# Gate and up tiles of a SwiGLU layer as 2x2 blocks by Strassen's scheme, in a hybrid decoder step on Trainium2

## The chip, the cores and the metric

The program runs on one core of one Trainium2 chip. The metric is the device time of one execution in microseconds. The kernel before takes 1314.66 us, the median of three runs (1313.83 to 1316.19). TensorE multiplies, VectorE (DVE), ScalarE (ACT) and GpSimd (POOL) work on tiles of 128 partitions, and SyncE (SP) issues most loads.

## The reference

One layer of a hybrid decoder for 512 prompt tokens and 8 sample tokens with the same weights: windowed attention and RWKV-7 time mixing beside each other, merged by gates, one output projection, then a SwiGLU layer. The change concerns the last two lines before the final norm:

```python
x = x + (merged @ w_out)                                 # 1024 x 1024
hn = rms_norm(x, norm_ffn)
ffn = (silu(hn @ w_gate) * (hn @ w_up)) @ w_down         # 1024 -> 2816 -> 1024
y = rms_norm(x + ffn, norm_final)
```

All is in fp32.

## The kernel before

Activations lie transposed: a feature is a partition, the 520 tokens are columns, in two chunks of CH = 260 (`CS`). A product has 8 k-tiles (KD) of 128 features for 1024 inputs. The 2816 hidden features make 22 tiles (KF); each has a gate tile and an up tile of the weights, 128 x 8 x 128 numbers, and the two together are called a pair here.

TensorE multiplies in fp32r, so each fp32 operand is split into a high part and a rest, and a k-tile costs three matmuls: high x high, high weight x rest, rest of the weight x high (`gemm_chunk`, L535). A weight tile is loaded as `raw` by SP (`wraw`, L512), cast to `whi` by ACT and subtracted to `wlo` by DVE (`wsplit`, L521). So a gate or up tile is 2 chunks x 8 k-tiles x 3 = 48 matmuls of 260 columns, and a pair 96.

The multiplications are a list of `Job`s (L455; the list from L1916 on), which `play` (L549) runs one after another; in the second step of a job it loads the weights of the job after next and splits those of the next one. Each chunk takes one of three PSUM banks with the name `mm`; there are three more with the name `ax` and two `ch`.  When a chunk's product is complete, the job's `post` reads it out on DVE or ACT and so empties the bank.

The order on each engine is the order in which the program records its instructions. Other work (`norm2`, L1761, and `final`) runs as generators beside `play`; `Weave.run` (L433) decides at each `yield` who records next, by a model of the engines' clocks (`Clocks`, L226). All instructions are recorded through one helper, so the profile has them all on L380, and tiles are told apart by their names.

Around the change: `wo_pre` (L1721) loads the residual x2 (8 POOL DMAs) for the output projection, `wo_post` (L1746) adds the product to x2 and makes x2 times the norm's weight as a split pair in the places K0 to 21 of the tiles `fh` and `fl`. The norm's scale per token is not known before all of x2 is there. So the first EARLY = 3 pairs are multiplied with that unscaled vector, and the results are multiplied by the scale (`rsf`) in `gt_post` and `up_post`. Meanwhile `norm2` computes the scale, multiplies (`hf`) and splits the scaled vector per k-tile into `h2h` (ACT) and `h2l` (alternately DVE and POOL); all later pairs use these. For gate: `sl` = (tanh(g/2) + 1) x g; for up: `sl` x u; then half of it is split into `fh` and `fl`, which the down tiles read.

Of the kernel before, what the change touches and what calls it, by code (L numbers as in the profile page):

```python
# [42 lines left out]
EARLY = 3  # L43
# [422 lines left out]
def program(tc, I, O):  # L466
# [82 lines left out]
    def play(jobs, more=None):  # L549
        raws, ws = {0: first_raw, 1: second_raw}, {0: first_w}  # L550
# [1167 lines left out]
    mctx, fctx = ExitStack(), ExitStack()  # L1718
    ff = {}

    def wo_pre():  # L1721
        rctx.close()
        gctx.close()
        xp = pool("x2", ctx)
        ff["x2"] = x2 = xp.tile([128, KD, NT], FP, name="x2")
        for k in range(KD):
            G.dma_start(out=x2[:, k], in_=I["xT"][:, k])
# [18 lines left out]
    def wo_post(n):  # L1746
        def post(ps):
            x2 = ff["x2"]
            for c in range(2):
                V.tensor_tensor(out=x2[:, n, CS[c]], in0=x2[:, n, CS[c]], in1=ps[c][:, :CH], op=ALU.add)  # L1750

            g = feat[:, F_FFN, n:n + 1]
            S.activation(out=ff["h"][:, K0 + n], in_=x2[:, n], func=AF.Copy, scale=g)
            V.scalar_tensor_tensor(out=ff["l"][:, K0 + n], in0=x2[:, n], scalar=g, in1=ff["h"][:, K0 + n].bitcast(FP),
                                   op0=ALU.mult, op1=ALU.subtract)
            sumsq(ff["acc"], x2[:, n], n)
            if n == KD - 1:
                wv.spawn(norm2())
        return post

    def norm2():  # L1761
        mctx.close()
        hp2 = ff["hp2"] = pool("h2", h2ctx, side="right")
        hh2 = ff["hh"] = hp2.tile([128, KD, NT], FR, name="h2h")
        hl2 = ff["hl"] = hp2.tile([128, KD, NT], FR, name="h2l")
# [4 lines left out]
        for k in range(KD):  # L1770
# [4 lines left out]
            wv.set("h2", k)  # L1775
            yield (hl2[:, k],)
# [3 lines left out]
    def up_x(n):  # L1780
        return lambda: ([ff["h"][:, K0 + k] for k in range(KD)], [ff["l"][:, K0 + k] for k in range(KD)]) \
            if n < EARLY else (ff["hh"], ff["hl"])

    def gt_post(n):
        def post(ps):
            xp = ff["xp"]
            t = ff["t", n] = xp.tile([128, NT], FP, name=nm("sl"), tag="sl", bufs=2)
            for c in range(2):
                g = ps[c][:, :CH]
                if n < EARLY:  # L1790
                    gs = xp.tile([128, CH], FP, name=nm("g0"), tag="g0")
                    V.tensor_tensor(out=gs[:], in0=g, in1=ff["rs"][:, CS[c]], op=ALU.mult)
                    g = gs[:]
                S.activation(out=t[:, CS[c]], in_=g, func=AF.Tanh, scale=0.5)
                V.scalar_tensor_tensor(out=t[:, CS[c]], in0=t[:, CS[c]], scalar=1.0, in1=g, op0=ALU.add, op1=ALU.mult)
        return post

    def up_post(n):
        def post(ps):
            t = ff["t", n]  # L1800
            for c in range(2):
                V.tensor_tensor(out=t[:, CS[c]], in0=t[:, CS[c]], in1=ps[c][:, :CH], op=ALU.mult)
            if n < EARLY:
                V.tensor_tensor(out=t[:], in0=t[:], in1=ff["rs"][:], op=ALU.mult)
            S.activation(out=ff["h"][:, n], in_=t[:], func=AF.Copy, scale=0.5)
            V.scalar_tensor_tensor(out=ff["l"][:, n], in0=t[:], scalar=0.5, in1=ff["h"][:, n].bitcast(FP),
                                   op0=ALU.mult, op1=ALU.subtract)
        return post

# [106 lines left out]
    for n in range(KF):  # L1916
        rest.append(Job(I["w_gate"][n], KD, up_x(n), gt_post(n), hold=(lambda: wv.until("rs2")) if n == 0 else None,
                        bank=cbank if n == 0 else None, need={k: ("h2", k) for k in range(KD)} if n == EARLY else {}))
# [17 lines left out]
    for n in range(KD - 1):  # L1936
        for k0 in range(0, KF, 8):
            nk = min(8, KF - k0)
            rest.append(Job(I["w_down"][n][:, k0:k0 + nk], nk, down_x, down_post(n) if k0 + nk == KF else None, k0=k0,
                            first=(k0 == 0), last=(k0 + nk == KF), pre=down_pre if n == 0 and k0 == 0 else None))  # L1940

    for c in range(2):
        for k0 in range(0, KF, 8):
            nk = min(8, KF - k0)
            rest.append(Job(I["w_down"][KD - 1][:, k0:k0 + nk] if c == 0 else None, nk, down_x,
# [4 lines left out]
    wv.run(play(jobs, more))  # L1950
# [17 lines left out]
```

## Time and profile before

| | us |
|---|---|
| median of three runs | 1314.66 |
| profiled execution | 1316.53 |
| its span | 1314.8 |
| TensorE busy | 1264.7 |
| DVE busy | 843.7 |
| ACT busy | 610.6 |
| POOL busy | 175.0 |

The span is what the trace covers of the profiled execution, from the first instruction to the last. Busy times of different engines lie beside each other; a share over the whole span is a mean over stages. The mean granted clock of TensorE in the span is 0.98. In the trace, matmuls of 260 columns start some 0.12 us apart and are shown 0.28 us long, since they are pipelined. A row of the timeline has start, duration, engine, line, operation, output<-inputs with shapes, and in brackets the idle time of the engine before it with what ended it.

### The profile page before, as it was taken

Reading aid. Unit: us, or ns where it says so; the run is one execution under the profiler, and the core shown is the slowest. Engines: PE = TensorE matmul, PEld = TensorE weight load, DVE = VectorE, ACT = ScalarE, POOL = GpSimd, SP = SyncE. Lnnn points to the kernel's source line nnn. Section 1 sums busy time; section 2 is a strip of 40 time slices with the busy share of each in tenths; the row PEclk is TensorE's granted clock in tenths of the full one; section 3 lists DMA queues with packets and bytes.
Section 4 is the critical chain, followed back from the end, with each engine's and each line's share of the span. In section 5 each row is a group of like instructions: output and inputs, shape, how many; then the busy total and the mean of one; then the engine's idle time right before and its main releaser. Section 6 shows DMA issues by size and latency. Waiting matters only on the chain.

```text
span 1314.8 us, 29468 instructions
## 1 busy us (share of the span) xinstructions
PE 1264.7 (96%) x11738; PEld 1197.5 (91%) x11738; DVE 843.7 (64%) x2221; ACT 610.6 (46%) x1554; POOL 175.0 (13%) x261
## 2 busy tenths in 40 slices
PE   7999999999989989999999999999999999999996
PEld 7998999989978878888888888999999999999996
DVE  6956866954869998886986665555843444332333
ACT  5244244366656656675785665334433232222220
POOL 1300100100223332121123122110200000000000
PEclk9999999999989999997999999999999999999998
DMA  6523654634245554543245454552222222223331
GB/s 215 158 94 96 213 178 146 221 112 172 69 131 136 152 147 141 143 156 97 77 139 168 123 175 157 182 192 85 81 97 97 97 89 89 97 93 89 89 101 65
DMA packets 92137, 169.48 MB, mean 129 GB/s; under 512 B 42416, under 2 KB 47568, under 8 KB 92000
## 3 DMA queue, kind: packets, MB, share of 16 engines
q1 hardware_dynamic: 60880, 102.46, 24.6%
q0 software_dynamic: 14512, 46.47, 11.5%
q10 hardware_dynamic: 16608, 18.68, 4.3%
q8 instruction: 92, 1.51, 0.5%
q14 instruction: 45, 0.37, 0.1%
HBM read 133.20 MB, written 27.94 MB: 123 GB/s over the span
## 4 chain that ended last, share of the span: by engine, by line
PE 64%; DVE 15%; issue 9%; DMA 6%; ACT 4%; POOL 1%; SPq 1%; ACTq 0%; DVEq 0%; POOLq 0%
PE mm L380 51%; PE ax L380 8%; PE ch L380 5%; DVE wlo L380 2%; DVE X L380 1%; DVE xt L380 1%; DMA fb<-FD 1%; DMA sw<-raw 1%; ACT KB L380 1%; DVE k L380 1%; DMA raw<-w_in 1%; SPq L380 1%; DVE raw L380 1%; DVE qk L380 1%; DVE GH L380 1%
## 5 line engine op out<-in xcount | busy, mean ns | idle before, releaser
L380 PE MATMUL mm<-hh,whi 128*128 128x260 f32 x1136 | 340.2, 299 | 0.8 <-ACT gt L380 0.8
L380 PE MATMUL mm<-hh,wlo 128*128 128x260 f32 x1136 | 325.4, 286 | 4.3 <-DVE wlo L380 4.3
L380 PE MATMUL mm<-hl,whi 128*128 128x260 f32 x1136 | 325.7, 287 | 0.0
L380 ACT CAST whi<-raw 128x1024 fp32r<-128x1024 f32 (+1 forms) x165 | 170.1, 1032 | 324.4 <-PE mm L380 290.6
L380 DVE TENSOR_TENSOR wlo<-raw,whi 128x1024 fp32r<-128x1024 f32 (+1 forms) x165 | 197.9, 1199 | 140.2 <-ACT whi L380 137.0
L380 PEld LDWEIGHTS mm<-hh,whi 128*128 128x128 f32 x1136 | 215.7, 190 | 13.3 <-issue 6.0
L380 PEld LDWEIGHTS mm<-hh,wlo 128*128 128x128 f32 x1136 | 215.4, 190 | 6.5 <-DVE wlo L380 5.8
L380 PEld LDWEIGHTS mm<-hl,whi 128*128 128x128 f32 x1136 | 215.5, 190 | 1.4 <-issue 0.2
L380 PE MATMUL mm<-h2l,whi 128*128 128x260 f32 x608 | 171.5, 282 | 0.0
L380 PE MATMUL mm<-h2h,wlo 128*128 128x260 f32 x608 | 171.4, 282 | 0.0
L380 PE MATMUL mm<-h2h,whi 128*128 128x260 f32 x608 | 171.4, 282 | 0.0
L380 PEld LDWEIGHTS mm<-h2h,wlo 128*128 128x128 f32 x608 | 114.5, 188 | 0.0
L380 PEld LDWEIGHTS mm<-h2l,whi 128*128 128x128 f32 x608 | 114.4, 188 | 0.0
L380 PEld LDWEIGHTS mm<-h2h,whi 128*128 128x128 f32 x608 | 114.4, 188 | 0.0
L380 PE MATMUL mm<-fh,wlo 128*128 128x260 f32 x388 | 109.6, 282 | 0.0
L380 PE MATMUL mm<-fh,whi 128*128 128x260 f32 x388 | 109.5, 282 | 0.0
L380 PE MATMUL mm<-fl,whi 128*128 128x260 f32 x388 | 109.5, 282 | 0.0
L380 PEld LDWEIGHTS mm<-fh,whi 128*128 128x128 f32 x388 | 73.1, 188 | 0.0
L380 PEld LDWEIGHTS mm<-fl,whi 128*128 128x128 f32 x388 | 73.0, 188 | 0.0
L380 PEld LDWEIGHTS mm<-fh,wlo 128*128 128x128 f32 x388 | 72.9, 188 | 0.0
L380 DVE TENSOR_TENSOR xt<-X,LT 128x60 f32<-128x60 f32 (+24 forms) x248 | 60.3, 243 | 3.6
L380 DVE TENSOR_TENSOR X<-X,xt 128x60 f32<-128x60 f32 (+24 forms) x248 | 57.6, 232 | 3.8
(390 smaller groups left out, 2588.8 us busy)
## 6 DMA issues: line engine op xcount, KB each, us to landing
raw<-w_in SPq DMA_DIRECT2D x77, 512.0 KB, 3.7
raw<-w_gate SPq DMA_DIRECT2D x22, 512.0 KB, 3.2
raw<-w_up SPq DMA_DIRECT2D x22, 512.0 KB, 3.2
raw<-w_down SPq DMA_DIRECT2D x16, 512.0 KB, 3.5
kt<-kcache POOLq DMA_DIRECT2D x24, 256.0 KB, 3.7
kt<-vcache POOLq DMA_DIRECT2D x24, 256.0 KB, 3.5
sw<-raw ACTq DMA_DIRECT2D x64, 65.0 KB, 3.6
GD<-gt ACTq DMA_DIRECT2D x16, 260.0 KB, 3.0
```

What stands on the lines that cost most here:

```text
L380: r = f(*a, **k)
```

## The change

EARLY becomes 4. The pairs 4 to 21 leave the job list for a new generator `pairs`. Of these 18, the pairs 4, 7, 10, 13, 16 and 19 stay plain and are done in four units (gate and up, each in two halves of four k-tiles) of 24 matmuls. The other twelve are taken as a 2x2 block product: rows are the gate tile and the up tile, the inner dimension is the two halves of the k-tiles (A and B), columns are the two chunks. Strassen's scheme in Winograd's form has seven products of 12 matmuls instead of eight, four sums of weight blocks, four sums of blocks of the hidden vector, and seven sums of results. All sums are on DVE.

`norm2` works on pairs of k-tiles j and j + 4: two scaled vectors, one split of four blocks, four block differences, one split of these, each split over 4 x 260 = 1040 columns by one ACT cast and one DVE subtraction; POOL has no part of it. Weights are split per unit, in halves of 512 columns, into four half slots, three units ahead; weight sums are written into `accf`, `rsf` and over the raw tiles. Units take the three `mm` and three `ax` banks by turns. Raw weights of every other pair come into two tiles of their own. To make room, x2 is written to DRAM in `wo_post` (8 POOL DMAs) and loaded again when the down tiles begin (8 POOL DMAs), and part of `fh`/`fl` is made later in memory that x2 had (`fz`).

The diff, cut to its core:

```diff
-EARLY = 3
+EARLY = 4
...
     def wo_post(n):
...
+            G.dma_start(out=X2D[:, n], in_=x2[n])
...
     def norm2():
...
-        for k in range(KD):
-            t = ff["xp"].tile([128, NT], FP, name=nm("hf"), tag="sq", bufs=2)
-            V.scalar_tensor_tensor(out=t[:], in0=ff["x2"][:, k], scalar=feat[:, F_FFN, k:k + 1], in1=ff["rs"][:],
-                                   op0=ALU.mult, op1=ALU.mult)
-            split(hh2[:, k], hl2[:, k], t[:], (V, G)[k % 2])
+        for j in range(KD // 2):
+            z = ff["fp"].tile([128, 8, CH], FP, name=nm("z"), tag=f"z{j % 2}")
+            for i in range(2):
+                k = j + i * KD // 2
+                V.scalar_tensor_tensor(out=z[:, 2 * i:2 * i + 2], in0=ff["x2"][k].rearrange("p (b c) -> p b c", b=2),
+                                       scalar=feat[:, F_FFN, k:k + 1], in1=ff["rs"][:].rearrange("p (b c) -> p b c", b=2),
+                                       op0=ALU.mult, op1=ALU.mult)
+            split(hh2[:, j, :4], hl2[:, j, :4], z[:, :4])
+            for o, x, y in ((4, 1, 0), (6, 3, 1), (5, 3, 4), (7, 2, 5)):
+                V.tensor_tensor(out=z[:, o], in0=z[:, x], in1=z[:, y], op=ALU.subtract)
+            yield (z[:, 7],)
+            split(hh2[:, j, 4:], hl2[:, j, 4:], z[:, 4:])
...
+    def pairs():
...
+        for n in range(EARLY, KF):
+            if (n - EARLY) % 3:
+                units += [(n, True, w, ((b, w, True, True),)) for w, b in enumerate((0, 5, 2, 6, 7, 4, 3))]
+            else:
+                units += [(n, False, w, tuple((b, 2 * (w // 2) + c, w % 2 == 0, w % 2 == 1) for c, b in
+                                              enumerate(((0, 1), (2, 3))[w % 2]))) for w in range(4)]
...
+            out, x, y, op = {1: (s2, s1, g[:, A], ALU.subtract), 3: (u[:, A], g[:, A], u[:, A], ALU.subtract),
+                             6: (g[:, A], g[:, B], s2, ALU.subtract)}.get(w, (None,) * 4)
+            if w == 1:
+                V.tensor_tensor(out=s1, in0=u[:, A], in1=u[:, B], op=ALU.add)
+            if out is not None:
+                V.tensor_tensor(out=out, in0=x, in1=y, op=op)
...
+                S.copy(out=hi, in_=src)
+                V.tensor_tensor(out=lo, in0=src, in1=hi.bitcast(FP), op=ALU.subtract)
...
+            if w == 0:
+                S.copy(out=p, in_=o)
+            elif w == 1:
+                plus(q, p)
+            elif w == 2:
+                plus(p, p)
+                silu2(t[:, CS[0]], p)
+            elif w == 3:
+                plus(r, q)
+            elif w == 4:
+                plus(p, r)
+                V.tensor_tensor(out=t[:, CS[0]], in0=t[:, CS[0]], in1=p, op=ALU.mult)
+            elif w == 5:
+                plus(q, q)
+                plus(r, r)
+            else:
+                plus(q, q)
+                silu2(t[:, CS[1]], q)
+                V.tensor_tensor(out=t[:, CS[1]], in0=t[:, CS[1]], in1=r, op=ALU.mult)
+                half_out(n, t)
...
+        for q in range(3):
+            prep(q)
...
+            prep(q + 3)
...
-    wv.run(play(jobs, more))
+    def everything():
+        yield from play(jobs, {0: first_raw, 1: second_raw}, {0: first_w}, more)
+        yield from pairs()
+        yield from play(down, down_raw, down_w)
+    wv.run(everything())
```

In the order on DVE before, one pair of the long stretch (a row has the line, the operation, output<-inputs and the shape; `mm` are products in PSUM):

```order
L380 TENSOR_TENSOR wlo_13316<-raw_13252,whi_13315 128x1024
L380 SCALAR_TENSOR_TENSOR sl_13295<-sl_13295,mm_13270 128x260
L380 TENSOR_TENSOR sl_13295<-sl_13295,mm_13300 128x260
L380 TENSOR_TENSOR sl_13295<-sl_13295,mm_13331 128x260
L380 TENSOR_TENSOR wlo_13376<-raw_13313,whi_13375 128x1024
L380 SCALAR_TENSOR_TENSOR fl<-sl_13295,fh 128x520
```

In the new order on DVE, about half of a block pair (`pq` are the accumulated results, `mm` and `ax` the products in PSUM, `accf`, `rsf` and `raw` on the left are sums of weight blocks):

```order
L380 TENSOR_TENSOR wlo_13270<-raw_13598,whi_13269 128x512
L380 TENSOR_TENSOR pq_13797<-pq_13797,ax_13815 128x260
L380 TENSOR_TENSOR wlo_13270<-accf,whi_13269 128x512
L380 TENSOR_TENSOR accf<-raw_13673 128x512
L380 TENSOR_TENSOR pq_13797<-pq_13797,mm_13831 128x260
L380 TENSOR_TENSOR wlo_13268<-raw_13597,whi_13267 128x512
L380 SCALAR_TENSOR_TENSOR sl_13796<-sl_13796,pq_13797 128x260
L380 TENSOR_TENSOR pq_13798<-pq_13797,ax_13854 128x260
L380 TENSOR_TENSOR wlo_13268<-raw_13672,whi_13267 128x512
L380 TENSOR_TENSOR rsf<-accf,raw_13672 128x512
L380 TENSOR_TENSOR pq_13797<-pq_13798,mm_13870 128x260
```

Rests of weights and sums of results stand by turns, the sums of weights of the next pair among them.

In the early stretch, before, DVE's rows from the weight rest at 925.83 us to the first product of up tile 0 (`mm_12777`; `g` is a gate product times the scale):

```order
L380 TENSOR_TENSOR wlo_12793<-raw_12712,whi_12792 128x1024
L380 SCALAR_TENSOR_TENSOR hf_12746<-x_12155,feat,rsf 128x520
L380 TENSOR_TENSOR g_1889_12769<-ch_12699,rsf 128x260
L380 SCALAR_TENSOR_TENSOR hf_12796<-x_12155,feat,rsf 128x520
L380 TENSOR_TENSOR h2l<-hf_12746,h2h 128x520
L380 SCALAR_TENSOR_TENSOR sl_12768<-sl_12768,g_1889_12769 128x260
L380 SCALAR_TENSOR_TENSOR hf_12837<-x_12155,feat,rsf 128x520
L380 TENSOR_TENSOR g_1890_12773<-ch_12730,rsf 128x260
L380 TENSOR_TENSOR sl_12768<-sl_12768,mm_12777 128x260
```

And in the new order the same stretch (the product is `mm_12794`; `z` are the blocks and their sums):

```order
L380 TENSOR_TENSOR wlo_12810<-raw_12724,whi_12809 128x1024
L380 SCALAR_TENSOR_TENSOR z_12758<-x_1833_12165,feat,rsf 128x520
L380 SCALAR_TENSOR_TENSOR z_12758<-x_1834_12166,feat,rsf 128x520
L380 TENSOR_TENSOR z_12758<-z_12758 128x260 x3
L380 TENSOR_TENSOR g_1895_12786<-ch_12711,rsf 128x260
L380 TENSOR_TENSOR h2l<-z_12758,h2h 128x1040
L380 TENSOR_TENSOR z_12758<-z_12758 128x260
L380 SCALAR_TENSOR_TENSOR sl_12785<-sl_12785,g_1895_12786 128x260
L380 SCALAR_TENSOR_TENSOR z_12888<-x_1833_12165,feat,rsf 128x520
L380 TENSOR_TENSOR g_1896_12790<-ch_12742,rsf 128x260
L380 TENSOR_TENSOR h2l<-z_12758,h2h 128x1040
L380 SCALAR_TENSOR_TENSOR sl_12785<-sl_12785,g_1896_12790 128x260
```

The next row reads `mm_12794`. Two rests of 1040 columns and the four sums of z now stand ahead of it, in place of one rest of 520 and one scaled vector of 520.

More of the change, by code (lines that the diff above doesn't have):

```diff
@@ L1716, in pb_post @@
         return post
-    mctx, fctx = ExitStack(), ExitStack()
+    mctx, fctx, sctx = (ExitStack() for _ in range(3))
+    X2D = drp.tile([128, KD, NT], FP, name="X2D")
     ff = {}
@@ L1731, in wo_pre @@
         fp = pool("ff", fctx)
-        ff["h"] = fp.tile([128, KF, NT], FR, name="fh")
-        ff["l"] = fp.tile([128, KF, NT], FR, name="fl")
+        for x in "hl":
+            a, b = (fp.tile([128, n, NT], FR, name=nm("f" + x)) for n in (EARLY, KF - EARLY - 8))
+            ff[x] = [a[:, k] for k in range(EARLY)] + [None] * 8 + [b[:, k] for k in range(KF - EARLY - 8)]
+        ff["fp"] = fp
+        xs = [fp.tile([128, 8, CH], FP, name=nm("x2"), tag=f"x{i}") for i in range(2)]
+        ff["x2"] = x2 = [xs[k // 4][:, k % 4 * 2:k % 4 * 2 + 2].rearrange("p a b -> p (a b)") for k in range(KD)]
+        for k in range(KD):
+            G.dma_start(out=x2[k], in_=I["xT"][:, k])
         yield ()
@@ L1763, in norm2 @@
         hp2 = ff["hp2"] = pool("h2", h2ctx, side="right")
-        hh2 = ff["hh"] = hp2.tile([128, KD, NT], FR, name="h2h")
-        hl2 = ff["hl"] = hp2.tile([128, KD, NT], FR, name="h2l")
+        hh2 = ff["hh"] = hp2.tile([128, KD // 2, 8, CH], FR, name="h2h")
+        hl2 = ff["hl"] = hp2.tile([128, KD // 2, 8, CH], FR, name="h2l")
         banks = yield from norm_r(ff["xp"], [ff["acc"]], slice(0, NT), TB, "f")
@@ L1769, in norm2 @@
         wv.set("rs2")
[L1770 to L1776 removed]
+        for j in range(KD // 2):
[10 more added lines that the diff above has]
+            split(hh2[:, j, 4:], hl2[:, j, 4:], z[:, 4:])
+            wv.set("h2", j)
+            yield (hl2[:, j],)
+        for i, x in enumerate("hl"):
+            for o, y in ((EARLY, "z"), (EARLY + 4, "x")):
+                w = ff["fp"].tile([128, 8, CH], FR, name=nm("fz"), tag=f"{y}{i}")
+                ff[x][o:o + 4] = [w[:, 2 * k:2 * k + 2].rearrange("p a b -> p (a b)") for k in range(4)]
+        ff["wp"] = pool("ws", sctx)
+        wv.set("ws")
     h2ctx = ExitStack()
     def up_x(n):
[L1781 to L1782 removed]
+        return lambda: (ff["h"][K0:], ff["l"][K0:])
     def gt_post(n):
@@ L1915, in program @@
         rest.append(Job(I["w_out"][n], KD, lambda: (mrg["h"], mrg["l"]), wo_post(n), pre=wo_pre if n == 0 else None))
-    for n in range(KF):
+    for n in range(EARLY):
         rest.append(Job(I["w_gate"][n], KD, up_x(n), gt_post(n), hold=(lambda: wv.until("rs2")) if n == 0 else None,
-                        bank=cbank if n == 0 else None, need={k: ("h2", k) for k in range(KD)} if n == EARLY else {}))
+                        bank=cbank if n == 0 else None))
         rest.append(Job(I["w_up"][n], KD, up_x(n), up_post(n)))
@@ L1922, in down_x @@
         return ff["h"], ff["l"]
+    down, down_raw, down_w = [], {}, {}
     def down_pre():
+        sctx.close()
         h2ctx.close()
+        ff["x2"] = pool("x2b", ctx, side="right").tile([128, KD, NT], FP, name="x2b")
+        for k in range(KD):
+            G.dma_start(out=ff["x2"][:, k], in_=X2D[:, k])
         yield ()
@@ L1938, in program @@
             nk = min(8, KF - k0)
-            rest.append(Job(I["w_down"][n][:, k0:k0 + nk], nk, down_x, down_post(n) if k0 + nk == KF else None, k0=k0,
+            down.append(Job(I["w_down"][n][:, k0:k0 + nk], nk, down_x, down_post(n) if k0 + nk == KF else None, k0=k0,
                             first=(k0 == 0), last=(k0 + nk == KF), pre=down_pre if n == 0 and k0 == 0 else None))
@@ L1944, in program @@
             nk = min(8, KF - k0)
-            rest.append(Job(I["w_down"][KD - 1][:, k0:k0 + nk] if c == 0 else None, nk, down_x,
+            down.append(Job(I["w_down"][KD - 1][:, k0:k0 + nk] if c == 0 else None, nk, down_x,
                             down_post(KD - 1, (c,)) if k0 + nk == KF else None, k0=k0, first=(k0 == 0),
```

117 lines of the change are left out of this document (97 added, 20 removed).

## The prediction

> **What bounds the kernel now.** I first read the page's busy line and its slices, then a table of the stages, then the timeline of VectorE in one pair of gate and up tiles. The busy line of the page:
>
> ```profile
> PE 1264.7 (96%) x11738; PEld 1197.5 (91%) x11738; DVE 843.7 (64%) x2221; ACT 610.6 (46%) x1554; POOL 175.0 (13%) x261
> ```
>
> The 96% is a mean over stages, so the stages decide. The table of stretches (length, then busy time and count of PE, PEld, DVE, ACT, POOL, then granted clock, DMA share, GB/s):
>
> ```profile
> 820.00:871.00 51.00, 49.61 (x409) 48.79 (x408) 29.04 (x53) 15.26 (x22) 7.51 (x14) 1.00 0.53 177
> 871.00:917.00 46.00, 46.00 (x387) 45.92 (x386) 25.39 (x39) 17.26 (x23) 4.23 (x8) 1.00 0.40 139
> 917.00:926.00 9.00, 8.87 (x75) 8.46 (x74) 4.94 (x16) 3.85 (x6) 0.00 (x0) 1.00 0.17 58
> 926.00:954.30 28.30, 28.30 (x238) 28.30 (x238) 26.18 (x38) 12.34 (x21) 6.81 (x4) 1.00 0.24 85
> 954.30:1172.00 217.70, 217.70 (x1827) 217.70 (x1827) 89.41 (x134) 63.02 (x95) 0.00 (x0) 1.00 0.27 93
> 1172.00:1290.00 118.00, 118.00 (x987) 118.00 (x986) 36.37 (x45) 26.73 (x31) 0.00 (x0) 1.00 0.29 87
> ```
>
> Up to 917 the orders of both kernels agree; 917 to 954 is pairs 0 to 2; 954.3 to 1172 is pairs 3 to 21, 19 of them with 96 matmuls each (1824; the row counts 1827); then come the down tiles. From 926 to 1290 TensorE is busy all the time at clock 1.00. DVE works 89.41 of 217.70 us in the long stretch (41%), ACT 63.02, POOL nothing, DMA 27%. There a matmul less is time less, as long as DVE's added work finds its place. In 926 to 954.3, however, DVE is already busy 26.18 of 28.30 us.
>
> One pair in the long stretch, from the timeline of DVE (start, duration, ..., in brackets the idle time before and what ended it):
>
> ```profile
> 992.29 0.43 DVE L380 SCALAR_TENSOR_TENSOR sl<-sl,mm 128x260 f32<-128x260 f32 x1 [0.54 <-ACT sl L380]
> 995.67 1.23 DVE L380 TENSOR_TENSOR wlo<-raw,whi 128x1024 fp32r<-128x1024 f32 x1 [2.96 <-ACT whi L380]
> ...
> 997.54 0.43 DVE L380 TENSOR_TENSOR sl<-sl,mm 128x260 f32<-128x260 f32 x1 [0.30 <-PE mm L380]
> 1000.39 0.43 DVE L380 TENSOR_TENSOR sl<-sl,mm 128x260 f32<-128x260 f32 x1 [2.43 <-PE mm L380]
> ...
> 1003.75 0.42 DVE L380 SCALAR_TENSOR_TENSOR sl<-sl,mm 128x260 f32<-128x260 f32 x1 [0.55 <-ACT sl L380]
> ```
>
> The same instruction returns after 1003.75 - 992.29 = 11.46 us, so a matmul costs 11.46/96 = 0.1194 us. DVE waits for others in every gap; nobody waits for it.
>
> **What goes: 144 matmuls.** Pairs 4 to 21 are 18 pairs of tiles, six plain and twelve in 2x2 blocks. A block pair has 7 products of 4 k-tiles x 3 = 12 matmuls, 84 in place of 96. The order shows the same: 144 matmuls fewer on TensorE. 144 x 0.1194 = 17.19 us, if TensorE stays without idle time. The Trainium skill ("TensorE: Matmul & The Clock Gate", section "Back-to-back issue gap") has an isolated gap of N/2.4 + 2.5 ns, 110.8 ns for 260 columns, which would make the saving 15.96 us, an estimate from that page; it adds that sustained streams run below this at N=512. The row above is a sustained stream at 0.1194 us, so the row decides.
>
> **What comes on DVE in a block pair.** Durations overlap between neighbours, so I take the distance from start to start of instructions that follow each other without idle time:
>
> ```profile
> 940.17 0.41 DVE L380 TENSOR_TENSOR g<-mm,rsf 128x260 f32<-128x260 f32 x1
> 940.51 1.21 DVE L380 TENSOR_TENSOR wlo<-raw,whi 128x1024 fp32r<-128x1024 f32 x1
> 941.64 0.41 DVE L380 SCALAR_TENSOR_TENSOR sl<-sl,g 128x260 f32<-128x260 f32 x1
> 941.98 1.80 DVE L380 SCALAR_TENSOR_TENSOR hf<-x,feat,rsf 128x520 f32<-128x520 f32 x1
> 943.70 0.41 DVE L380 TENSOR_TENSOR sl<-sl,mm 128x260 f32<-128x260 f32 x1
> 944.04 0.75 DVE L380 SCALAR_TENSOR_TENSOR hf<-x,feat,rsf 128x520 f32<-128x520 f32 x1
> 944.71 0.69 DVE L380 TENSOR_TENSOR h2l<-hf,h2h 128x520 fp32r<-128x520 f32 x1
> 945.32 0.41 DVE L380 TENSOR_TENSOR sl<-sl,mm 128x260 f32<-128x260 f32 x1
> ```
>
> 260 columns take 0.34 (940.17 to 940.51), 520 take 0.61 (944.71 to 945.32), 1024 take 1.13 (940.51 to 941.64), a scaled 520 takes 0.67 (944.04 to 944.71). No row has 512 columns: between 0.34 and 0.61, I take 0.60, nearest to 520. A block pair then costs DVE 7 weight rests x 0.60 + 4 weight sums x 0.60 + 7 output sums x 0.34 + 4 silu and product steps x 0.34 + the final rest 0.61 = 10.95 us, beside 84 x 0.1194 = 10.03 us of TensorE. It is over by 0.92. A plain pair has 4 x 0.60 + 4 x 0.34 + 0.61 = 4.37 us beside 11.46. Three pairs together: DVE 2 x 10.95 + 4.37 = 26.3 us, TensorE 2 x 10.03 + 11.46 = 31.5 (34.4 before). So the sum fits only over three pairs, with DVE 1.8 us behind after two block pairs and 7 us of slack in the plain one. Weight halves are split three products ahead, each with 12 x 0.1194 = 1.43 us, together 4.3 us, and I followed the new order instruction by instruction with these durations: every weight rest is ready 1.9 us or more before TensorE asks for it. The rotation of the six PSUM banks gives no wait there. ACT's steps are, by the rows of the tile h2h and of a group of the long stretch (median, then mean ns),
>
> ```profile
> L380 ACT CAST h2h<-hf x8: 627/628/630, 927.8 to 944.8; 128x520 fp32r<-128x520 f32 x8
> L380 ACT ACTIVATE sl<-mm 128x260 f32<-128x260 f32 x38 | 14.6, 385 | 27.4 <-PE mm L380 27.4
> ```
>
> 7 casts x 0.63 + the copy and two tanh x 0.39 + the final cast 0.63 = 6.2 us of a block pair's 10.03; I cost it at nothing, DVE being the fuller one. The weights are the same bytes, and DMA was at 27%. Term: 0, bounds 0 and +2.
>
> **What comes in the early stretch.** The blocks of the hidden vector and their sums are made while pairs 0 to 3 run: per two k-tiles, two scaled 520s (1.34), four sums (1.36) and two rests of 1040 columns (some 1.15 each by the slope from 520 to 1024), 5.0 us, and four times that 20. Before, DVE had eight scaled 520s and four rests of 520, 7.8 us, and POOL the other four rests. So 12 us more on an engine that was full. POOL's share leaves, and with it its contention with DVE:
>
> ```profile
> 940.99 2.23 POOL L380 TENSOR_TENSOR h2l<-hf,h2h 128x520 fp32r<-128x520 f32 x1 [4.53 <-ACT h2h L380]
> 945.53 1.31 POOL L380 TENSOR_TENSOR h2l<-hf,h2h 128x520 fp32r<-128x520 f32 x1 [2.31 <-ACT h2h L380]
> ```
>
> Beside the first of these the scaled 520 of 941.98 took 1.80 instead of 0.75. DVE stays full from 926 on, now to about 965, 12 us past the old end of the stretch; the fourth early pair lies there. The wait that this makes is that for a PSUM bank. Pairs before 954.37 go half a tile (24 matmuls, 2.87 us) after another:
>
> ```profile
> 925.83 1.23 DVE L380 TENSOR_TENSOR wlo<-raw,whi 128x1024 fp32r<-128x1024 f32 x1 [1.66 <-PE ch L380]
> 931.67 0.41 DVE L380 TENSOR_TENSOR sl<-sl,mm 128x260 f32<-128x260 f32 x1
> ...
> 954.25 0.28 PE L380 MATMUL mm<-fh,wlo 128*128 128x260 f32 x1
> 954.37 0.28 PE L380 MATMUL mm<-h2h,whi 128*128 128x260 f32 x1
> ```
>
> The second half of gate tile 1 begins seven halves before 954.37, at 934.3, and needs the bank that DVE's first product of up tile 0 empties. Before, that stood at 931.67. Now two rests of 1040 and three sums stand ahead of it; added up from 925.83 in the new order, with ACT's casts, it ends at 934.4 to 934.7. The next such reads come out at 940.3 against 940.1 and at 943.6 against 942.9. So 0.7 us in the first half of the stretch, and I take 0.6 for the like in the second: 1.3 us. Bounds: 0 (the 1.80 rows were contention and are gone, which could make DVE earlier by 1.05 each) and 4 (every read of the four pairs late by half a microsecond).
>
> **The seams.** The loads of pair 4 are issued among the w_out tiles, where they wait for the end of another product, and those behind them wait as long anyway: 0. X2 is written out and reloaded by POOL's queue in 16 DMAs, while POOL has nothing else (0.00 in the table) and the reload has the whole of the first down tiles to come in: 0. The first down tile's weight rest stands among the last output sums, by the new order and the durations above with some 0.4 us in hand: 0, bound 1.
>
> **Sum.** 17.19 - 1.3 = 15.9 us. The profiled execution took 1316.53 (span 1314.8 and 1.7 around it), 1.87 above the median 1314.66 of the three runs, and would become 1300.6; the median becomes **1298.8**. The costs' ends are 0 and 4 + 2 + 1 = 7, which gives 1297.5 to 1304.5; the three runs spread by 0.8 below the median and 1.5 above it (1313.83 to 1316.19).
>
> **Rivals.** *DVE sets the pace in block pairs.* For it: 10.95 against 10.03, and a price for 512 columns that no row shows. If the plain pair's slack were lost, twelve block pairs would take 10.95: the gain is 17.2 - 1.3 - 12 x 0.92 = 4.9, 1309.8. Against: work can be done 4.3 us ahead. Chance 0.04.
>
> *The early stretch and the seams cost more.* Bank waits of 4 in pairs 0 to 3 and another 4 at the two seams: gain 17.2 - 8 = 9.2, 1305.5. For: DVE was 93% busy there and gets a longer chain. Against: POOL's contention goes. Chance 0.10.
>
> *Slower: DVE's waits aren't filled.* In the pair above DVE waited 0.54 and 0.55 for tanh and 0.30 for a product, in order, with work behind it. An output sum can only go once its product has ended, and behind it stands the weight rest of a later product. If each block pair kept two waits of 0.55 and seven of 0.30, it would need 10.95 + 3.2 = 14.15 us, 4.12 over TensorE's time. Two in a row are 8.24 over, the lead of 1.9 is eaten, and each trio stalls 6.3 us, which the plain pair cannot give back: 6 x 6.3 = 38 against 15.9, so 1336.8. It is slower when six stalls exceed 15.9, 2.65 a trio: 2 x (p - 10.03) - 1.9 > 2.65, p over 12.3 us, hence 1.35 us of waits that stay unfilled in a pair. Against it: weight rests and output sums alternate in the new order, so a late product holds up only work that has four microseconds. Chance 0.06.
>
> *Slower: the clock.* Seven short products with banks that change more often could leave gaps that lower the granted clock. In the rows above it is 1.00 also where TensorE idles (49.61 of 51 us busy, 8.87 of 9), so nothing shows it at such gaps; yet it would cost much: the 12 x 84 + 6 x 96 = 1584 matmuls of pairs 4 to 21 take 189.1 us, and break even with the old 206.3 at clock 0.917. At 0.78, the clock of this row of the table,
>
> ```profile
> 1290.00:1315.00 25.00, 13.80 (x121) 13.29 (x119) 10.84 (x40) 0.84 (x2) 0.00 (x0) 0.78 0.25 86
> ```
>
> it would be 53 us more, 1352. Chance 0.02. The Trainium skill has such a rule (same page, "A second HAM failure mode: psum-queue depth-cycling": TensorE that idles briefly between groups as it cycles through PSUM banks makes the gate swing between two clocks); the trace bears it out only in that 0.78 stands where TensorE is busy 13.80 of 25 us.
>
> **How the numbers follow.** The forecast has 0.78; 1305.5 has 0.10, 1309.8 has 0.04, the slower ones 0.06 and 0.02. The range goes from 1296.5 (the whole 17.2 and the runs' own 0.8 below) to 1306.0, which takes in the case at 1305.5; with the costs short of their ends the forecast alone would be 1297 to 1302, but that leaves out more than 2 in 10. A measurement can tell some 0.2%, 2.6 us. All but the two slower cases are faster by more: 0.92; no change needs the third rival at just its break-even, 0.01 of its 0.06; slower 0.07.
>
> **What would show it.** Right: TensorE at clock 1.00 and without idle time from the fourth pair on, three pairs in 31.5 us, the 512 rows of DVE near 0.60 from start to start, DVE about 84% busy in the trios; waits of TensorE for DVE's reads of 0.2 to 1 us between 930 and 965. Wrong: TensorE waiting for a weight rest within block pairs (first or third rival, told apart by whether DVE itself is idle then), a granted clock below 0.95 there, waits over 4 us in the early stretch.

## The result, and the profile after

The changed kernel takes 1296.91 us, the median of four runs (1296.4 to 1299.81), beside 1315.43 us of the kernel before on the same chip (four runs, 1313.83 to 1318.43). The ratio is 0.9861, 95% interval 0.9838 to 0.9885. On a second chip, six runs of the changed kernel gave 0.9871 (0.9822 to 0.9921). The forecast was 1298.8, faster.

The busy line of the page after, answering to the one of before:

```profile
PE 1246.1 (96%) x11594; PEld 1178.2 (91%) x11594; DVE 933.4 (72%) x2448; ACT 648.2 (50%) x1638; POOL 176.0 (14%) x273
```

11738 matmuls became 11594, 144 fewer, and 18.6 us of TensorE's busy time went; DVE gained 90 us. Where that lies is read from three stretches with sharp ends on TensorE: from the first early matmul to the first one that reads `h2h`, from there to the first down matmul, and from there to the first matmul of the final norm (the first with `accf` as operand). Of before, then of after (length, busy and count of PE, PEld, DVE, ACT, POOL, clock, DMA share, GB/s):

```profile
917.11:954.37 37.26, 37.13 (x311) 36.73 (x309) 31.12 (x53) 16.19 (x26) 6.81 (x4) 1.00 0.23 80
954.37:1171.99 217.62, 217.62 (x1826) 217.62 (x1825) 89.41 (x134) 63.02 (x95) 0.00 (x0) 1.00 0.27 93
1171.99:1290.60 118.61, 118.61 (x992) 118.61 (x991) 36.37 (x45) 26.73 (x31) 0.00 (x0) 1.00 0.29 86
```

```profile
915.77:965.51 49.74, 49.26 (x406) 48.41 (x405) 45.39 (x86) 23.23 (x32) 0.54 (x1) 1.00 0.28 91
965.51:1155.34 189.83, 189.83 (x1586) 189.83 (x1585) 162.87 (x327) 93.19 (x172) 0.00 (x0) 1.00 0.29 92
1155.34:1274.15 118.81, 118.81 (x992) 118.81 (x991) 37.53 (x49) 27.07 (x32) 4.25 (x8) 1.00 0.34 107
```

The first stretch has three pairs before and four after. The three together went from 373.49 to 358.38: 15.11 us gained in these stretches. TensorE is busy all of the 189.83 us and at clock 1.00, while DVE now works 162.87 of them, 86% in place of 41%.

The medians differ by 18.5 us, 3.4 more than the stretches. The spans of the two profiled runs differ by 16.8: 1.34 us more lie ahead of the stretches and 0.35 behind them. The rest of the 18.5 stands in no profile, but single runs differ by more than that ahead of 915 us, where the orders of the two kernels agree. Two of the experiments below show how far that goes; the stretch before their first early matmul:

```profile
0.00:904.40 904.40, 867.37 (x8502) 801.46 (x8503) 676.21 (x1949) 502.66 (x1400) 171.17 (x264) 0.99 0.49 151
```

```profile
0.00:922.70 922.70, 880.19 (x8502) 813.74 (x8503) 676.19 (x1949) 503.28 (x1400) 171.32 (x264) 0.98 0.49 148
```

The same 8502 matmuls and the same work of DVE, 18.3 us apart, the longer one at the lower granted clock. So the experiments are compared by the stretches, which repeat within 0.02 us (the changed kernel run a second time had 49.73, 189.82 and again 118.81), and by whole times only where these were taken in rounds.

The block pairs themselves, from DVE's timeline in the first block pair after a plain one:

```profile
980.14 0.42 DVE L380 TENSOR_TENSOR pq<-pq,ax 128x260 f32<-128x260 f32 x1 [0.24 <-PE ax L380]
...
983.61 0.68 DVE L380 TENSOR_TENSOR wlo<-raw,whi 128x512 fp32r<-128x512 f32 x1
984.21 0.68 DVE L380 TENSOR_TENSOR rsf<-accf,raw 128x512 f32<-128x512 f32 x1
984.81 0.42 DVE L380 TENSOR_TENSOR pq<-pq,mm 128x260 f32<-128x260 f32 x1
985.15 0.68 DVE L380 TENSOR_TENSOR raw<-raw,raw 128x512 f32<-128x512 f32 x1
985.75 0.42 DVE L380 TENSOR_TENSOR sl<-sl,pq 128x260 f32<-128x260 f32 x1
```

An instruction of 512 columns takes 0.60 us from start to start (983.61 to 984.21), the value that had no row before. After the first wait of 0.24 DVE pauses for no more than 0.1 us at a time up to the plain pair: it is behind, as worked out. In the next plain pair it comes free again:

```profile
1003.66 0.69 DVE L380 TENSOR_TENSOR wlo<-rsf,whi 128x512 fp32r<-128x512 f32 x1 [0.46 <-ACT whi L380]
...
1006.54 0.69 DVE L380 TENSOR_TENSOR wlo<-raw,whi 128x512 fp32r<-128x512 f32 x1 [1.85 <-ACT whi L380]
...
1008.82 0.42 DVE L380 TENSOR_TENSOR sl<-sl,ax 128x260 f32<-128x260 f32 x1 [1.00 <-PE ax L380]
```

And the early stretch: the two longest waits that it has not had before, from TensorE's timeline:

```profile
932.77 0.28 PE L380 MATMUL mm<-fh,wlo 128*128 128x260 f32 x1
933.13 0.39 PE L380 MATMUL mm<-fh,whi 128*128 128x260 f32 x1
...
941.87 0.28 PE L380 MATMUL mm<-fh,wlo 128*128 128x260 f32 x1
942.40 0.36 PE L380 MATMUL mm<-fh,whi 128*128 128x260 f32 x1 [0.26 <-DVE g L380]
```

Where matmuls otherwise start 0.12 apart, these start 0.36 and 0.53 apart: 0.24 and 0.41 us lost, each at the first matmul into a bank that DVE has to empty.

### The profile page after: what moved, and what is told of

Same layout as the page of the kernel before. It is cut to its first block, busy times and chain, and to the rows that moved or that the text cites. A ratio compares the mean times of both kernels' runs of the same rounds, so it can differ in the third digit from the quotient of the medians.

```text
span 1298.0 us, 29596 instructions
## 1 busy us (share of the span) xinstructions
PE 1246.1 (96%) x11594; PEld 1178.2 (91%) x11594; DVE 933.4 (72%) x2448; ACT 648.2 (50%) x1638; POOL 176.0 (14%) x273
## 3 DMA queue, kind: packets, MB, share of 16 engines
q0 software_dynamic: 15792, 50.73, 12.9%
## 4 chain that ended last, share of the span: by engine, by line
PE 59%; DVE 18%; issue 11%; DMA 6%; ACT 4%; POOL 2%; SPq 0%; ACTq 0%; DVEq 0%; POOLq 0%
PE mm L380 39%; PE ax L380 15%; PE ch L380 5%; DVE wlo L380 3%; DMA fb<-FD 1%; DVE X L380 1%; DVE xt L380 1%; DMA kt<-vcache 1%; DVE qk L380 1%; DVE raw L380 1%; DMA sw<-raw 1%; DVE sw L380 1%; DVE k L380 1%; DVE GH L380 1%; DVE oac L380 1%
## 5 line engine op out<-in xcount | busy, mean ns | idle before, releaser
L380 ACT CAST whi<-raw 128x1024 fp32r<-128x1024 f32 (+2 forms) x213 | 184.2, 866 | 255.8 <-PE mm L380 185.0
L380 DVE TENSOR_TENSOR wlo<-raw,whi 128x1024 fp32r<-128x1024 f32 (+2 forms) x213 | 211.5, 993 | 86.4 <-ACT whi L380 81.7
L380 PE MATMUL mm<-fh,wlo 128*128 128x260 f32 x308 | 87.1, 283 | 0.0
L380 PE MATMUL mm<-fl,whi 128*128 128x260 f32 x308 | 87.1, 283 | 0.0
L380 PE MATMUL mm<-h2l,whi 128*128 128x260 f32 x264 | 74.8, 283 | 0.0
L380 PE MATMUL mm<-h2h,wlo 128*128 128x260 f32 x264 | 74.6, 282 | 0.0
L380 PE MATMUL mm<-h2h,whi 128*128 128x260 f32 x264 | 74.6, 282 | 0.0
L380 PE MATMUL ax<-h2h,wlo 128*128 128x260 f32 x264 | 74.5, 282 | 0.0
L380 PE MATMUL ax<-h2l,whi 128*128 128x260 f32 x264 | 74.5, 282 | 0.0
L380 PE MATMUL ax<-h2h,whi 128*128 128x260 f32 x264 | 74.3, 281 | 0.0
```

The lines of the kernel that those rows point to most:

```text
L380: r = f(*a, **k)
```

## The experiments

My theory is that of the forecast: TensorE sets the time, a matmul less is 0.12 us less, and DVE's sums are hidden as long as its lag within a run of block pairs stays inside the lead. The rivals are that DVE sets the pace already, that something else than the matmuls makes the gain, and that the lead does not matter. In the table are the stretches of all kernels, measured as above:

| kernel | block pairs | early | pairs | down |
|---|---|---|---|---|
| changed | 12 | 49.74 | 189.83 | 118.81 |
| all plain | 0 | 49.72 | 206.62 | 118.81 |
| all blocks | 18 | 49.70 | 208.55 | 120.28 |
| fourteen | 14 | 49.73 | 189.81 | 118.81 |
| one ahead | 12 | 49.73 | 189.83 | 118.81 |
| two slots, halves overwritten | 12 | 49.72 | 199.12 | 118.81 |
| two slots, one ahead | 12 | 49.71 | 200.96 | 119.59 |
| weight sums on POOL | 12 | 49.73 | 190.62 | 119.96 |
| early rest on POOL | 12 | 51.90 | 189.83 | 118.80 |
| sixteen, silu | 16 | 48.78 | 187.81 | 119.73 |
| fourteen, silu | 14 | 48.77 | 187.03 | 118.81 |
| fifteen, silu | 15 | 48.76 | 185.63 | 118.85 |

**All plain.**

```diff
-            if (n - EARLY) % 3:
+            if False:
```

> All eighteen pairs go through the new code in its plain form: half weight tiles three units ahead, six PSUM banks by turns, x2 written out and reloaded, block sums of the hidden vector still made (and not used), four early pairs; only the seven-product form is gone, so TensorE has the matmuls of the kernel before. My theory (the gain is the 144 matmuls, all else costs about 1 us): 1296.9 + 12 x (96 x 0.1194 - 84 x 0.1204) = 1296.9 + 16.2 = 1313, within 2 us of the kernel before. Rival (a good part of the gain comes from what else changed, from the two raw tiles more, the three units of lead or the early loads): clearly under 1310. Rival (the new structure costs several us that the blocks then win back): over 1318.

Measured: 206.62 us of pairs, 16.79 more than the changed kernel; the ratio to the kernel before is 1.0031 (0.9997 to 1.0066, ten runs). The three stretches add up to 375.15 us beside 373.49 before. So the new structure alone brings nothing, and the 144 matmuls make the whole gain. The row shows TensorE busy throughout and DVE back at 90 us:

```profile
954.98:1161.60 206.62, 206.62 (x1730) 206.62 (x1729) 90.15 (x162) 67.38 (x125) 0.00 (x0) 1.00 0.26 87
```

**All blocks.**

```diff
-            if (n - EARLY) % 3:
+            if True:
...
-                o = (q if q < last - 4 else q - last) % 4
+                o = (q - last) % 4
```

(The second edit only moves the rotation of the four half slots, so that it ends as before with another number of units; it is in all the kernels below with another number of block pairs.)

> No pair stays plain: 18 block pairs, 72 matmuls fewer still. Theory that DVE then sets the pace: a block pair costs DVE 10.95 us by the rows (7 x 0.60 + 4 x 0.60 + 7 x 0.34 + 4 x 0.34 + 0.61) beside 10.11 of TensorE, so 18 x 10.95 = 197.1 in place of the 189.8 us from the first block matmul to the first down matmul, some 1304 us, and TensorE shows waits for weight rests adding up to about 15 us. Rival (only the matmuls count, DVE's excess of 0.84 a pair is absorbed somewhere): 72 x 0.12 = 8.6 us less, 1288. Rival (DVE's waits for products and tanh come on top, since the queue is in order): a pair over 12 us, 1325 or more.

Measured: 208.55 us, 18.7 more than with twelve, although 72 matmuls fewer are done; ratio to the kernel before 1.0044 (1.0013 to 1.0074), so the whole gain is gone. The first theory had the direction, but said 197. A block pair takes 208.55/18 = 11.59 us in the mean, 0.64 over the 10.95 worked out; from the third on, the rest of `rsf` returns every 11.7 us (983.10, 994.79, 1006.47). The row of the stretch, and the main waits of DVE and of TensorE in it (waiter, what it waited for, us in total, times, longest):

```profile
958.88:1167.43 208.55, 194.93 (x1515) 184.23 (x1513) 198.43 (x410) 102.23 (x197) 0.00 (x0) 1.00 0.26 84
```

```profile
DVE wlo L380 <- ACT whi L380: 7.6, 16, 0.7
```

```profile
PE ax L380 <- ACT whi L380: 6.7, 16, 0.9
PE mm L380 <- ACT whi L380: 6.2, 15, 0.6
```

DVE works 198.43 of 208.55 us, so it is the fullest engine. But TensorE idles 13.6 us, and 12.9 of these are put down to casts of weights on ACT. DVE's own wait of some 0.48 us (7.6/16) comes back nearly once a pair, at the rest of the weight sum `rsf`. ACT's timeline shows where it comes from:

```profile
981.93 0.62 ACT L380 CAST whi<-raw 128x512 fp32r<-128x512 f32 x1 [2.92 <-PE mm L380]
982.45 0.61 ACT L380 CAST whi<-rsf 128x512 fp32r<-128x512 f32 x1
```

The cast of `rsf` stands behind another cast, which had waited 2.92 us for TensorE; in the order of the program it is that of a unit three further on, and it waits until TensorE has left its slot. So TensorE waits for casts, casts wait for TensorE's slots, and DVE waits for casts. Also, TensorE's matmuls no longer go unit by unit here (see the next experiment). How much of the 11.7 us comes from DVE's lag and how much from this order is not shown. The third rival of the prediction (waits that stay unfilled) is there, with 0.64 to 0.75 us a pair where it needed 1.35 to make the change slower.

**Fourteen.**

```diff
-            if (n - EARLY) % 3:
+            if (n - EARLY) % 5:
```

> Four block pairs to one plain pair (plain: 4, 9, 14, 19), 14 block pairs in all, 24 matmuls fewer. By the sums DVE needs 4 x 10.95 + 4.37 = 48.2 us a group and TensorE 4 x 10.11 + 11.5 = 51.9, so the mean fits, but DVE falls behind by 0.84 in each block pair, 3.4 in a run of four, of which the lead of about 1.9 us covers a part. Theory of the lead: 2 x 1.4 = 2.8 us gained less up to 1.5 stalled in each of three or four runs: 1294 to 1299, TensorE waiting for weight rests near the end of the fourth block pair and nowhere else. Rival (the mean alone decides): 1294 with no wait. Rival (DVE is at its limit already in two in a row): over 1302.

Measured: 189.81 us, the same as with twelve, though 24 matmuls are gone. The 2.8 us gained come back as waits of TensorE. They are short; one of 0.1 us stands in the third block pair of each run of four, the others in the fourth. One place in TensorE's timeline, and DVE's and ACT's at the same time:

```profile
997.42 0.33 PE L380 MATMUL mm<-h2h,whi 128*128 128x260 f32 x1
997.59 0.28 PE L380 MATMUL mm<-h2l,whi 128*128 128x260 f32 x1
997.71 0.28 PE L380 MATMUL ax<-h2h,whi 128*128 128x260 f32 x1
997.83 0.28 PE L380 MATMUL ax<-h2l,whi 128*128 128x260 f32 x1
998.22 0.39 PE L380 MATMUL ax<-h2h,whi 128*128 128x260 f32 x1
998.45 0.28 PE L380 MATMUL mm<-h2h,wlo 128*128 128x260 f32 x1
```

```profile
997.34 0.69 DVE L380 TENSOR_TENSOR wlo<-rsf,whi 128x512 fp32r<-128x512 f32 x1
997.95 0.68 DVE L380 TENSOR_TENSOR wlo<-raw,whi 128x512 fp32r<-128x512 f32 x1
998.55 0.42 DVE L380 TENSOR_TENSOR pq<-pq,mm 128x260 f32<-128x260 f32 x1
```

```profile
997.55 0.62 ACT L380 CAST whi<-raw 128x512 fp32r<-128x512 f32 x1 [0.23 <-PE ax L380]
```

The unit that starts at 997.42 needs its rest for its third matmul, which would be due at 997.66. The rest of 997.34 ends at 998.03, 0.4 us late, and DVE has no pause: the lag is real. But in the order of this kernel the first two matmuls of the next unit (997.71, 997.83) and one of a third unit (998.22) stand ahead of that third matmul. The one of 998.22 needs the cast of 997.55, which ends at 998.17 and had itself waited for TensorE to leave the slot; this is the 0.27 us lost, 998.22 standing that much further from 997.83 than the spacing of 0.12. Units are broken up in this way in fourteen, all blocks, both kernels with two slots and sixteen with silu. In the changed kernel and all others of the table the matmuls go to the banks in unbroken runs of 12. So what the lag costs, and what the order that came with it costs, are not told apart here.

That the waits give back just what two more block pairs gain is chance. The mean, 48.2 of 51.9 us by the sums, doesn't decide: it would have allowed fourteen. In runs of two, as in the change, no rest comes late.

**One ahead.**

```diff
-        for q in range(3):
-            prep(q)
+        prep(0)
...
-            prep(q + 3)
+            prep(q + 1)
```

> Weights are split one unit ahead instead of three, nothing else. DVE's sum is the same, 26.3 us of a trio's 31.6. If only the sum matters: 1297. If the lead carries it: the rest of a weight half stands behind the cast (0.63), a weight sum (0.60) and up to two output sums and a product step of the unit before (1.0), with 1.44 us for all, so TensorE waits 0.5 to 1 us in most of the 84 units of block pairs: 1340 to 1380, waits of TensorE on the weight rest at the head.

Measured: 189.83 us, not a wait more, where I expected 1340 us and above in all. But it doesn't tell what it was meant to: the built order on DVE has its weight rests within 0.8 us of the same places as before. One stands 13.70 us behind the first block-stage matmul in both, at 979.21 of the changed kernel (after 965.51) and at 980.71 here (after 967.01):

```profile
979.21 0.69 DVE L380 TENSOR_TENSOR wlo<-raw,whi 128x512 fp32r<-128x512 f32 x1
```

```profile
980.71 0.69 DVE L380 TENSOR_TENSOR wlo<-raw,whi 128x512 fp32r<-128x512 f32 x1
```

The recorded instructions are sorted once more by their modelled start; what holds a split back is a slot that isn't free, not the line at which it is called. The lead has to be taken away by slots.

**Two slots.** Two half slots for split weights in place of four, called three units ahead as in the change. Halves are then overwritten before their use, so this kernel does not multiply the right halves of the weights, but does the same amount of work.

```diff
-                o = (q if q < last - 4 else q - last) % 4
+                o = q % 2
```

> Two half slots for split weights instead of four, the rest as in the changed kernel: a weight half can only be split once TensorE is done with the half two units earlier, so the lead cannot exceed one unit, 1.44 us, whatever the order says. If the lead carries the scheme: cast 0.63, its start latency and the rest 0.60 have to fit behind the end of a unit, 1.3 to 1.5 us of 1.44, so TensorE waits in many of the 84 block units, by 0.2 to 0.8 each, and the stretch from the first block matmul to the first down matmul grows from 189.8 to between 205 and 255 us. If DVE's sum alone decides: 189.8, as with the split of one unit ahead.

**Two slots, one ahead.** The same, with the right weights.

```diff
-        for q in range(3):
-            prep(q)
+        prep(0)
...
-            prep(q + 3)
+            prep(q + 1)
...
-                o = (q if q < last - 4 else q - last) % 4
+                o = 2 + q % 2
```

> Two half slots for split weights and the split one unit ahead, so that the lead is truly one unit at most; the earlier two-slot kernel overwrote halves before their use, its stretch of 199.1 us is a time of the same work in an order that multiplies wrong halves. If the lead carries the scheme: the next half can be cast only when the unit before has left its slot, cast 0.63 and rest 0.60 and their starts against 1.44 us, with DVE's sums between: waits of 0.2 to 0.8 us in most of the 84 block units, 205 to 255 us from the first block matmul to the first down matmul. If DVE's sum alone decides: 189.8.

Measured: 199.12 and 200.96 us in place of 189.83, so with a lead of one unit 9.3 and 11.1 us are lost, more than half of the gain. That is less than the 15 to 65 expected. In the second kernel the waits are up to 0.45 us and run from the last unit of the first block pair of two through the second (984.06 to 996.01 in the first two); the plain pairs have none, and the first block pairs hardly any before that unit. The longest are for casts, TensorE's row and ACT's:

```profile
987.37 0.39 PE L380 MATMUL mm<-h2h,whi 128*128 128x260 f32 x1 [0.23 <-ACT whi L380]
```

```profile
986.69 0.62 ACT L380 CAST whi<-rsf 128x512 fp32r<-128x512 f32 x1 [0.26 <-DVE rsf L380]
...
991.11 0.62 ACT L380 CAST whi<-raw 128x512 fp32r<-128x512 f32 x1 [0.59 <-PE ax L380]
...
992.74 0.62 ACT L380 CAST whi<-accf 128x512 fp32r<-128x512 f32 x1 [0.63 <-PE mm L380]
```

The cast that TensorE waits for at 987.37 had waited for DVE's sum `rsf`: DVE is behind, and no lead is left. The casts of 991.11 and 992.74 wait for TensorE to leave a slot. Such waits of ACT stand in the changed kernel too (0.82 us ahead of a cast at 981.45) and cost nothing there. So the lead carries a good part of the scheme, and the four slots are what gives it.

**Weight sums on POOL.** All four sums of a block pair go to POOL.

```diff
-                V.tensor_tensor(out=s1, in0=u[:, A], in1=u[:, B], op=ALU.add)
+                G.tensor_tensor(out=s1, in0=u[:, A], in1=u[:, B], op=ALU.add)
...
-                V.tensor_tensor(out=out, in0=x, in1=y, op=op)
+                G.tensor_tensor(out=out, in0=x, in1=y, op=op)
```

> The four weight sums of each block pair are made on POOL, which has nothing else there, instead of DVE. If the engines only add: DVE has 8.55 us a block pair, still hidden, and the stretch stays at 189.8 us. Contention theory, from the rows of before where a VectorE instruction of 0.75 us took 1.80 beside POOL's: each sum takes POOL 1.3 to 2.2 us and delays DVE by about 1.05, so a block pair costs DVE 8.55 + 4.2 = 12.75 us beside 10.07 of TensorE, 5.4 over in two, of which the lead covers 2: about 3 us of waits a trio, 205 to 212 us for the stretch.

Measured: 190.62 us, 0.8 more, and 1.15 more at the seam to the down tiles. The contention is there, and it isn't worth 205. DVE lost 2.4 us of work a block pair and yet was busy longer:

```profile
960.05:1150.67 190.62, 190.62 (x1586) 190.08 (x1585) 174.38 (x281) 90.29 (x172) 66.02 (x46) 1.00 0.29 93
```

174.38 in place of 162.87. So moving work to an idle engine made the busy one busier, by (174.38 - 162.87)/12 = 0.96 us a block pair; my estimate had 1.8 (12.75 beside 10.95). The lag stayed just inside the lead: in the second block pair the rest of `rsf` ends at 983.26, and the first matmul that reads it starts at 983.31; TensorE loses 0.15 us there, once in every two block pairs.

**Early rest on POOL.**

```diff
-            split(hh2[:, j, 4:], hl2[:, j, 4:], z[:, 4:])
+            split(hh2[:, j, 4:], hl2[:, j, 4:], z[:, 4:], G)
```

> In the early stretch the rest of the four block differences (128x1040) goes to POOL, as every second rest went before the change. The stretch from the first early matmul to the first block matmul is 49.74 us in the changed kernel, 1.0 over four plain pairs of before. If POOL relieves DVE (4 x 1.15 us less): 48.7 to 49.5. If it costs DVE more by contention than it takes over (a POOL rest of 1040 columns at 2.6 to 4 us, DVE delayed by a microsecond and more beside each): 50 to 53, DVE rows of 1.8 us again in the timeline.

Measured: 51.90 us, 2.16 more than the changed kernel, as the second theory says; 2.0 of it is one wait of TensorE:

```profile
PE mm L380 <- DVE wlo L380: 2.0, 1, 2.0
```

POOL's four rests of 1040 columns took 2.44 to 3.49 us, and beside each of them one row of DVE took 2.15 to 3.13 us where its like takes 0.70 to 1.23. DVE was busy 47.42 us of the stretch beside 45.39 in the changed kernel, with four rests less to do. The weight rest that TensorE waited for also stands later in this kernel's order, so how much of the one wait is contention is not shown. In the stretch where DVE is full, giving work to POOL cost more than it took. That the change took POOL out of this stretch is part of why it cost only 1.0 us.

**Fewer steps on DVE.** If the lag of DVE is what stops more block pairs, taking work from DVE must allow them. The silu of the gate was a tanh on ACT and a product on DVE; here it is one function on ACT, and the later factor 0.5 falls away. That takes two instructions of 0.34 from each pair. The plain pairs are every ninth, fifth and sixth.

```diff
-        S.activation(out=t, in_=g, func=AF.Tanh, scale=0.5)
-        V.scalar_tensor_tensor(out=t, in0=t, scalar=1.0, in1=g, op0=ALU.add, op1=ALU.mult)
+        S.activation(out=t, in_=g, func=AF.Silu)
...
-            if (n - EARLY) % 3:
+            if (n - EARLY) % 9:      # % 5 with fourteen, % 6 with fifteen
```

> Sixteen block pairs (plain: 4 and 13), and the two steps tanh on ACT and (t + 1) x g on DVE become one silu on ACT, which takes 0.68 us a pair from DVE: 10.27 beside 10.07 of TensorE. 48 matmuls fewer than the changed kernel, 5.7 us. If DVE's own work were all that counts, it falls behind by 0.2 a pair, 1.6 in eight, within the lead: the stretch is 189.8 - 5.7 = 184.1 us. If the unfilled waits seen with eighteen block pairs stay (11.59 measured beside 10.95 worked out, 0.64 a pair): 10.91 a pair, 6.7 over in eight, less the lead of 2, twice: 193 us or more, no gain.

> Fourteen block pairs (plain: 4, 9, 14, 19) and silu in one step on ACT, which takes 0.68 us a pair from DVE. Without the silu, fourteen gave back their 2.9 us in waits for weight rests late in each run of four. With it DVE is 0.2 over TensorE a block pair instead of 0.88, 0.8 in a run of four, so the waits should go: stretch from the first block matmul to the first down matmul 189.8 - 2.9 = 186.9 us, the early stretch 48.8, together 3.8 us below the changed kernel, 1293 beside 1296.9. Rival (the waits have another cause than DVE's lag): 189.8 again.

> Fifteen block pairs in runs of five (plain: 4, 10, 16), with the silu on ACT. In the sixteen of before, the first wait of TensorE came late in the fifth block pair of a run. If the lag theory holds: 189.8 - 4.3 = 185.5 us and under 1 us of waits, 5 us below the changed kernel in all, some 1292. If waits grow as with sixteen (3.7 us): 187 to 189, no better than fourteen.

> The changed kernel itself beside the two, to compare on one chip: ratio to the kernel before 0.986 as measured, some 15 us in the three stretches of the feed-forward part.

Sixteen: 187.81 us beside the 184.1 and the 193 of the two theories; 2.0 us gained on twelve, with 3.7 us of waits. The first stands at 1035.25, in the sixth block pair of a run and not, as I had read it, in the fifth. Fourteen: 187.03, as the lag theory said (186.9), without a wait, where the same number without the silu had 189.81. Fifteen, in runs of five: 185.63, against 185.5, without a wait:

```profile
963.80:1149.43 185.63, 185.63 (x1550) 185.63 (x1549) 168.10 (x331) 97.89 (x184) 0.00 (x0) 1.00 0.29 95
```

The early stretch loses 1.0 us with the silu, to 48.77, four plain pairs of before (37.26 + 11.46 = 48.72): there too DVE was what TensorE waited for. In whole times, taken in rounds on one chip with 11 runs of the kernel before (median 1312.26): fifteen 1292.26 us, ratio 0.9842 (0.9799 to 0.9885); fourteen 1295.3, 0.9861 (0.9820 to 0.9901); the changed kernel 1298.21, 0.9871 (0.9822 to 0.9921). The intervals overlap; by the three stretches fifteen is 353.24 beside 358.37 of the changed kernel, 5.1 us below it, and by them it is the fastest of these kernels.

## Why the prediction was right

**The matmuls.** Predicted 17.19 us. From the first `h2h` matmul on the stretch shrank by 217.62 - 11.46 - 189.83 = 16.33, counting 18 pairs on each side. The all-plain kernel splits the rest: 206.62/18 = 11.48 us for a plain pair in place of 11.46, and (189.83 - 6 x 11.48)/12 = 10.08 for a block pair in place of 84 x 0.1194 = 10.03. So each block pair paid 1.40 us for twelve matmuls, and some 0.86 in all went to matmuls that stand a little further apart than before (0.1198 us in place of 0.1193). That was the term "if TensorE stays without idle time", 5% too large.

**DVE in the block pairs.** Right in its price (0.60 for 512 columns) and its total: 12 x 10.95 + 6 x 4.37 = 157.6 worked out, 162.87 busy. The 5.3 us between them are 3%. That it is hidden was right for two in a row; fourteen and eighteen show that it doesn't hold for any number.

**The lead.** The prediction had every weight rest ready 1.9 us or more before its use. That was right: matched in the order of the program, the smallest distance from the end of a rest to the start of the first matmul that reads it is 1.97 us in the changed kernel (1.98 in the first two block pairs, where the rest of 986.09 ends at 986.77 and its matmul starts at 988.75). It is 1.10 us with the call one unit ahead, where TensorE still waits for no rest, and 0.05 in the second kernel with two slots and in the one with the sums on POOL, where it does wait. What the prediction had wrong is the cause, "split three products ahead": most of the lead comes from the four slots. The call's place is worth 0.9 us of it, and with two slots the lead is one unit and 11.1 us are lost.

**The early stretch.** Predicted 1.3, measured 49.74 - 37.26 - 11.46 = 1.02. The first half was right in place: 934.3 and 942.9 in the timeline of before are 933.0 and 941.6 after the 1.34 us by which the profiled run was ahead here, and the waits are at 933.1 and 942.4. That half cost some 0.9 us in place of 0.7. The 0.6 for the second half was too much: after 942.6 TensorE loses next to nothing. That the sum came so near is in part luck.

**The seams.** Predicted 0; the down stretch became 0.20 longer, with its new DMAs beside it.

Together 16.33 - 1.02 - 0.20 = 15.11, against 15.9 forecast. The medians say 18.5, with 15 to 21 by the interval of the ratio, so they can't tell the two apart; that the median lies 1.9 us below the forecast says nothing about its terms.

**The rivals.** DVE's lag costs time in longer runs: with fourteen the first 0.1 us is lost in the third block pair in a row. The slower case asked for over 12.3 us a block pair; with eighteen it was 11.59 in the mean and 11.7 from the third on. The clock stayed at 1.00 through all the bank changes, so the Trainium skill's rule on depth-cycling ("TensorE: Matmul & The Clock Gate", section "A second HAM failure mode: psum-queue depth-cycling") did not bear here, with a new bank every 1.44 us; even in the all-blocks kernel, where TensorE is idle for 13.6 of 208.55 us, the row has 1.00.

## What to carry to other kernels

When work is moved from a full engine to one with time to spare, the mean over a cycle is a necessary condition only: work out how far the second engine falls behind in the longest run of heavy steps, and compare that with the lead that its buffers (not its place in the code) allow. Runs of four in place of two gave back all that they gained here; taking two small instructions a pair from the lagging engine then made runs of five free of waits. Look also at the order on the full engine: where it mixes units, a wait can belong to work that was put ahead. And an idle engine whose instructions hold up the full one is no good place for its work.

## What the runs showed of the hardware

A POOL instruction holds up DVE until its end, but only where DVE reads SBUF alone. With the weight sums on POOL, its timeline, then DVE's:

```profile
977.33 1.62 POOL L380 TENSOR_TENSOR rsf<-accf,raw 128x512 f32<-128x512 f32 x1
978.91 1.48 POOL L380 TENSOR_TENSOR raw<-raw,raw 128x512 f32<-128x512 f32 x1
```

```profile
977.73 1.51 DVE L380 SCALAR_TENSOR_TENSOR sl<-sl,pq 128x260 f32<-128x260 f32 x1
979.16 0.41 DVE L380 TENSOR_TENSOR pq<-pq,ax 128x260 f32<-128x260 f32 x1
979.50 1.44 DVE L380 TENSOR_TENSOR wlo<-raw,whi 128x512 fp32r<-128x512 f32 x1
980.86 0.41 DVE L380 TENSOR_TENSOR pq<-pq,mm 128x260 f32<-128x260 f32 x1
```

The product of 977.73, two operands in SBUF, is shown 1.51 us long instead of 0.42 and ends 0.29 after POOL's instruction; the rest of 979.50, 1.44 instead of 0.69, ends 0.55 after the next one. The sum of 979.16, with an operand in PSUM, runs in 0.41 in the middle of POOL's. It is so in the whole stretch: of the rests that began while POOL's instruction had over 0.3 us left, all 24 took 1.08 us or more, and none of the 19 sums from PSUM took over 0.43. The Trainium skill ("SBUF — State Buffer", section "Terms") says the same of the hold: the port pair that the two arbitrate for is locked for a whole instruction and "the loser fully blocks". I had priced each POOL instruction at 1.05 us of DVE's time, from one row of 1.80; in part since 7 of the 19 instructions that DVE keeps in a block pair have an operand in PSUM and run on, it came out at (174.38 - 162.87 + 12 x 2.4)/48 = 0.84.

A product of 12 matmuls into a bank of its own takes 1.44 us, and each of the twelve block pairs took 10.08 us in place of 10.03. The 0.05 us do not lie at the changes of the PSUM bank: from start to start the matmuls stand 0.1202 us apart at the 131 changes and 0.1198 within a unit, beside 0.1193 in the kernel before. What sets them further apart is not shown.
